# Moving two modulation pieces, one transpose block and two eviction orders in a one-core hybrid diffusion layer

## The chip, the cores and the metric

The kernel runs on one core of one Trainium2 chip. Its time is the device time of the execution in microseconds (us). Five engines work side by side: PE (TensorE, with its weight loads shown apart as PEld), DVE (VectorE), ACT (ScalarE), POOL (GpSimd) and SP (SyncE, which here only starts DMA transfers). Each engine runs its own instructions in its own order, and waits where an operand of another engine or a buffer is not ready.

Before the change three runs took 1248.82, 1251.52 and 1250.69 us, with a median of 1250.69 us.

## The reference

One layer of a diffusion backbone in float32: 512 latent tokens, 256 context tokens, width 1024. Cut to what the change touches:

```python
mod = silu(c) @ w_mod + b_mod                       # 6 x 1024: shifts, scales, gates
sh1, sc1, gt1, sh2, sc2, gt2 = split(mod, 6)
h_lat, h_ctx = modulate(x, norm1_g, sh1, sc1), modulate(ctx, norm1_g, csh1, csc1)
p_lat, p_ctx = h_lat @ w_in, h_ctx @ w_in
y_ssd = rmsnorm((ssd(conv_silu(xBC), dt) + d * xs) * silu(z), ssd_norm_g)     # 4 groups, 4 chunks of 128 tokens
y_att = window_ctx_attention(rope(q), rope(k), v, k_ctx, v_ctx, sink)
o = (sigmoid(g1) * (y_ssd @ w_o_ssd) + sigmoid(g2) * (y_att @ w_o_att)) @ w_out
x = x + gt1 * o
x = x + gt2 * (conv_ffn(modulate(x, norm2_g, sh2, sc2)))
return rmsnorm(x, final_g)
```

## The kernel before, in words

**Matrix products.** Every weight arrives as float32 in tiles of 128 x 1024 (512 KB). ACT casts such a tile to a high part (line 148, `whi<-wraw`), DVE subtracts it from the tile to get the low part (line 149, `wlo<-wraw,whi`), and activations are split in the same way. A product is then three matmuls for each of eight k blocks: lines 192 and 193 use the high weight, line 195 the low one. `gemm` walks k from 0 to 7; after k = 1, 4 and 7 it takes one function off the front of the list `BETWEEN` and runs it, which is how small work of another stage is put between the matmuls of a projection.

**Weight queue.** All weights go through one ring of three raw buffers (tag `raw`, tile `wraw`, line 144), in the order of the program. `run` asks for each weight one ahead of its use. SP issues the transfers in that order, and an issue waits until the buffer that it overwrites has been read: for a projection's weight by the subtraction of line 149, for a modulation piece by the second of its two accumulations of line 724. What follows on SP waits behind it.

**Modulation pieces.** `m_step(i)` reads a 512 KB piece of `w_mod` with two DVE operations (lines 722 or 724) that scale it by silu(c) and add it to `tm`. Every fourth piece adds four transposes on PE (line 728) and a sum on DVE (lines 730 and 731). Pieces 0 to 7 are placed in the four state-space groups (two each), 8 to 15 beside the branch projections `os_step(3)` to `os_step(7)`, 16 to 23 beside the five output projections `out_step(0)` to `out_step(4)`, and the other eight beside the feed-forward steps. `weave` spreads them evenly.

**Values.** `v_step` (line 825) forms the values and the time steps of six blocks of 128 tokens (four latent, two context) in six accumulators. For each k it runs all six blocks, so the six end together. Then ACT casts each accumulator (line 839) and copies its last 64 columns (line 841), and DVE subtracts (line 840), in the order of the blocks. The first score matmul of the attention (line 885) comes next on PE.

**State-space groups.** `ssd_steps(g)` works chunk by chunk. `chunk_out` ends with `late` (line 1541): four transposes add `dx` to the accumulator `yd` (line 1546), and DVE multiplies by the gate (line 1548, `zs`). `late` is not run at once. It is the last entry of `BETWEEN`, and `x_fn`, the projection of the next group that stands between the chunks, runs it inside its matmuls. `x_fn` itself appends two entries which transpose the convolved tile of the previous projection (`turn`, line 1346, taken out by the ACT copies of line 1389). With three empty entries ahead of it, `late` runs after k = 1 of the context half (256 tokens) of the projection, since the latent half takes the first three. The convolution of a projection is an ACT scale (1318), two DVE taps (1319, 1320), a tanh on ACT (1326) and a product on DVE (1327).

**Output projection.** `out_step(o)` needs the weight `wout` of its column block, all eight blocks of the merged branches (`mh` and `ml`, made by lines 1621 to 1624), and x. Column blocks 5 to 7 are formed last, in `out_last`, by halves of 256 tokens (lines 1691 to 1693, weights in `wlast`).

**The end.** `down_last` forms the last column block of the result by two halves. For half `u` `add` evicts it (line 1897), squares it on ACT (line 1705), sums squares by matmul (line 235), takes the root (DVE 245, POOL 246), spreads it by transposes (line 252), and `finish(u)` scales eight blocks of the result (DVE line 1880, for two of them POOL line 1878) and stores them by pairs (line 1882). The pairs alternate between SP and ACT as the engine that issues.

## Time and profile before

| view | what | value |
|---|---|---|
| run | profiled execution, its span | 1249.82 us, 1248.0 us |
| run | granted TensorE clock | 0.998 |
| page, 1 | PE busy, matmuls | 1233.6 us (99%), 6466 |
| page, 1 | DVE, ACT, POOL busy | 860.0, 655.8, 145.8 us |
| page, 4 | chain that ended last | PE 91%, DVE 4%, DMA 2% |
| stretches | 544 to 662 us (groups 1 and 2): PE busy | 116.54 of 118.00 us |
| stretches | 662 to 728 us (last group): PE busy | 66.00 of 66.00 us |
| stretches | 800 to 827 us (branch projections' end): PE busy | 27.00 of 27.00 us |
| stretches | 827 to 856 us (output projection): PE busy | 26.80 of 29.00 us |
| stretches | 827 to 856 us: DMA share, rate | 0.76, 240 GB/s |

In the view of the stretches a stage is read by itself: busy time of each engine, and how far the DMA engines were loaded. The view of waits names, for each line that stood idle, what ended the idleness. The timeline gives start, length, engine and line of each instruction; a bracket at the end of a row tells how long the engine was idle before it and what ended that.

### The profile page before, as it was taken

To read this page: it belongs to the slowest core of one execution; us is meant where nothing else is said; L and a number is where in the kernel's file an instruction comes from. 1 tells how busy PE (TensorE), PEld (TensorE's weight loads), DVE (VectorE), ACT (ScalarE), POOL (GpSimd) and SP (SyncE) were. 2 spreads that over 40 slices of the span, in tenths; PEclk is the share of its full clock that TensorE was granted. 3 is DMA by queue.
4 is the path that set the end of the run, shared out by engine and by line. 5 is a ranking of instruction groups with operands and counts; after the bars stand their busy time and mean duration, and the time that the engine had idled before them with its cause. 6 is when DMAs were issued, how large, how long until landed. Compare 5 with 4: busy or idle time off the path is not lost.

```text
span 1248.0 us, 17379 instructions
## 1 busy us (share of the span) xinstructions
PE 1233.6 (99%) x6466; PEld 1013.4 (81%) x6466; DVE 860.0 (69%) x1385; ACT 655.8 (53%) x1223; POOL 145.8 (12%) x145
## 2 busy tenths in 40 slices
PE   9999999999999999999999999999999999999997
PEld 6798888888888878777777788888888888888886
DVE  4857788888645697886977667676777767772333
ACT  4657788787445476575674752224544444442221
POOL 0000000000000152351552630000100000000000
PEclk9999999999999999999999999999999999999999
DMA  9643242222356336344365477775233333333331
GB/s 379 235 134 87 64 136 80 83 79 77 119 174 192 95 105 165 96 155 156 102 186 169 143 257 256 233 234 168 85 118 109 111 118 118 105 111 95 104 93 68
DMA packets 90997, 174.57 MB, mean 140 GB/s; under 512 B 7712, under 2 KB 43360, under 8 KB 90912
## 3 DMA queue, kind: packets, MB, share of 16 engines
q1 hardware_dynamic: 89680, 172.40, 44.1%
q8 instruction: 51, 0.84, 0.3%
q10 hardware_dynamic: 1232, 1.06, 0.2%
q14 instruction: 34, 0.28, 0.1%
HBM read 150.82 MB, written 17.11 MB: 135 GB/s over the span
## 4 chain that ended last, share of the span: by engine, by line
PE 91%; DVE 4%; DMA 2%; ACT 1%; POOL 1%; issue 1%; DVEq 0%; ACTq 0%; POOLq 0%
PE acc L192 21%; PE acc L193 21%; PE acc L195 21%; PE score L885 3%; PE po L934 3%; PE mis L524 2%; PE pt L921 2%; PE mis L1525 2%; PE mis L1430 1%; DMA wraw<-wout 1%; PE acc L1004 1%; PE acc L1005 1%; PE acc L1006 1%; PE mis L1447 1%; PE mis L1533 1%; PE acc L1821 1%
## 5 line engine op out<-in xcount | busy, mean ns | idle before, releaser
L149 DVE TENSOR_TENSOR wlo<-wraw,whi 128x1024 fp32r<-128x1024 f32 (+2 forms) x127 | 157.8, 1242 | 128.1 <-ACT whi L148 124.9
L148 ACT CAST whi<-wraw 128x1024 fp32r<-128x1024 f32 (+2 forms) x127 | 131.1, 1033 | 190.9 <-PE acc L193 147.6
L192 PE MATMUL acc<-hlh,whi 128*128 128x512 f32 x472 | 193.8, 411 | 0.0
L195 PE MATMUL acc<-hlh,wlo 128*128 128x512 f32 x472 | 185.0, 392 | 0.0
L193 PE MATMUL acc<-hll,whi 128*128 128x512 f32 x472 | 184.9, 392 | 0.0
L195 PE MATMUL acc<-mh,wlo 128*128 128x512 f32 x368 | 143.4, 390 | 0.5 <-DVE wlo L149 0.5
L192 PE MATMUL acc<-mh,whi 128*128 128x512 f32 x368 | 143.6, 390 | 0.0
L193 PE MATMUL acc<-ml,whi 128*128 128x512 f32 x368 | 143.2, 389 | 0.0
L195 PEld LDWEIGHTS acc<-hlh,wlo 128*128 128x128 f32 x472 | 88.6, 188 | 19.4
L192 PEld LDWEIGHTS acc<-hlh,whi 128*128 128x128 f32 x472 | 88.8, 188 | 17.9 <-issue 3.1
L193 PEld LDWEIGHTS acc<-hll,whi 128*128 128x128 f32 x472 | 88.9, 188 | 17.4 <-issue 2.4
L195 PEld LDWEIGHTS acc<-mh,wlo 128*128 128x128 f32 x368 | 69.1, 188 | 15.6 <-DVE wlo L149 1.2
L192 PEld LDWEIGHTS acc<-mh,whi 128*128 128x128 f32 x368 | 69.1, 188 | 14.7 <-ACT whi L148 0.4
L193 PEld LDWEIGHTS acc<-ml,whi 128*128 128x128 f32 x368 | 69.1, 188 | 14.1
L1432 POOL TENSOR_TENSOR st<-st,eT 128x512 f32<-128x512 f32 x24 | 28.9, 1203 | 440.7 <-ACT st L1449 426.4
L894 DVE CUSTOM_DVE_ANT_0 p<-score,winm,nsink 128x512 f32<-128x512 f32 (+1 forms) x64 | 51.8, 810 | 16.3 <-PE score L885 14.8
L1319 DVE SCALAR_TENSOR_TENSOR ta<-acc,half,ta 128x511 f32<-128x511 f32 (+1 forms) x66 | 43.8, 664 | 24.5 <-ACT ta L1318 24.4
L246 POOL TENSOR_TENSOR rs<-ms,phalf 128x2 f32<-128x2 f32 (+1 forms) x5 | 4.8, 956 | 478.5 <-DVE ms L245 478.5
L192 PE MATMUL acc<-fh,whi 128*128 128x512 f32 x154 | 60.0, 390 | 0.0
L193 PE MATMUL acc<-fl,whi 128*128 128x512 f32 x154 | 59.9, 389 | 0.0
L195 PE MATMUL acc<-fh,wlo 128*128 128x512 f32 x154 | 59.9, 389 | 0.0
L901 ACT ACTIVATE p<-p,mneg 128x512 f32<-128x512 f32 (+1 forms) x64 | 49.7, 777 | 16.1 <-DVE mneg L894 15.5
(377 smaller groups left out, 2888.8 us busy)
## 6 DMA issues: line engine op xcount, KB each, us to landing
wraw<-wup SPq DMA_DIRECT2D x44, 512.0 KB, 3.5
fb<-cs_d SPq DMA_DIRECT2D x32, 512.0 KB, 6.4
wraw<-wm SPq DMA_DIRECT2D x32, 512.0 KB, 3.8
wraw<-wx SPq DMA_DIRECT2D x24, 512.0 KB, 3.4
wm<-wm SPq DMA_DIRECT2D x16, 512.0 KB, 8.1
wraw<-wz SPq DMA_DIRECT2D x16, 512.0 KB, 3.5
wraw<-wos SPq DMA_DIRECT2D x16, 512.0 KB, 4.5
wraw<-wdn SPq DMA_DIRECT2D x16, 512.0 KB, 3.5
```

The source lines that it names most:

```text
L148: S.copy(hi[:, :n], r[:, :n])
L149: V.tensor_tensor(lo[:, :n], r[:, :n], raw(hi[:, :n]), ALU.subtract)
L192: T.matmul(ps, wh, xh[:, k0 + k, :], start=a, stop=False)
L193: T.matmul(ps, wh, xl[:, k0 + k, :], start=False, stop=False)
L195: T.matmul(ps, wl, xh[:, k0 + k, :], start=False, stop=b)
L524: T.matmul(ps, w[a], h[b], start=c == 1, stop=c % n == 0, skip_group_check=True)
L885: T.matmul(ps[:, o : o + len(z) * P], Q[h][:, b * P : (b + 1) * P], k[:, j, z[0] * P : (z[-1] + 1) * P], start=v == 0 and o % 512 in (0, P ...
L894: V.tensor_tensor_reduce(p[:, :w], d["ps"][i][:, o0 : o0 + w], m, op0=ALU.add, op1=ALU.min, scale=1.0, scalar=nsink[:, h : h + 1], accum_o ...
L901: S.activation(p, p, AF.Exp, bias=d["mneg"][:, i : i + 1], scale=-1.0, accum_out=d["den"][:, i : i + 1])
L934: T.matmul(d["po"], vst[:, cols[x], j, :], d[y][x], start=x == 0 and y == "pth", stop=x == c - 1 and y == "ptl")
L1319: V.scalar_tensor_tensor(o[:, 1:n], ps[:, 0 : n - 1], hcol(base_w, i), o[:, 1:n], ALU.mult, ALU.add)
L1432: G.tensor_tensor(h8(n), h8(s), bc64(eT[:, z0 : z0 + 8, c]), ALU.mult)
```

## The change

Four edits are made together. Code that comes later in the file moves down by up to 14 lines, so a line number of the kernel before answers to a slightly higher one after (1548 to 1550, 1880 to 1885).

1. `v_step` runs k = 0 to 5 over all six blocks as before, then finishes k = 6 and 7 block by block in the order 4, 5, 0, 1, 2, 3, and evicts in that order.
2. In groups 0 to 2 `late` has four empty entries ahead of it in place of three, and is one entry with `turn(1)`, followed by `turn`. So it runs after k = 4 of the context half in place of k = 1. `x_fn` adds its own entries only where the list is empty (group 0's projections), and then leaves the first place empty.
3. Group 3 takes four modulation pieces (6 to 9) in place of two. The branch projections take 10 to 17, the output projection 18 to 23: six in place of eight.
4. In `down_last` the second half's last block is evicted and squared in two pieces of 128 tokens; the first half's four stores are spread (two before the last eviction, one after it, one after the root); the second half is stored by seven transfers, all but one of a single block of 128 x 256, in the order 0, 1, 4, (2, 3), 5, 6, 7.

**PE and DVE in a chunk of a group.** The first rows are PE's before, in the context half of a projection: `late`'s transposes (1546) come after six of its 24 matmuls.

```order
L192 MATMUL acc<-hch,whi 128x256
L193 MATMUL acc<-hcl,whi 128x256
L195 MATMUL acc<-hch,wlo 128x256
L1546 MATMUL mis<-ident,dx 128x128 x4
L192 MATMUL acc<-hch,whi 128x256
L193 MATMUL acc<-hcl,whi 128x256
```

After the change they come behind nine more, directly ahead of the first `turn` (1347, formerly 1346).

```order
L192 MATMUL acc<-hch,whi 128x256
L193 MATMUL acc<-hcl,whi 128x256
L195 MATMUL acc<-hch,wlo 128x256
L1548 MATMUL mis<-ident,dx 128x128 x4
L1347 MATMUL mis<-ident,tc 128x128 x4
L192 MATMUL acc<-hch,whi 128x256
```

On DVE the gate's product `zs` stood between the two taps of the latent convolution (1319 and 1320) before:

```order
L1517 TENSOR_TENSOR E<-E,mis 128x512 x2
L1319 SCALAR_TENSOR_TENSOR ta<-acc,half,ta 128x511
L1548 TENSOR_TENSOR zs<-mis,zs 128x4x128
L1320 SCALAR_TENSOR_TENSOR ta<-acc,half,ta 128x511
L1327 SCALAR_TENSOR_TENSOR tc<-tb,ta 128x512
```

and stands behind both now:

```order
L1519 TENSOR_TENSOR E<-E,mis 128x512 x2
L1320 SCALAR_TENSOR_TENSOR ta<-acc,half,ta 128x511
L1321 SCALAR_TENSOR_TENSOR ta<-acc,half,ta 128x511
L1550 TENSOR_TENSOR zs<-mis,zs 128x4x128
L1328 SCALAR_TENSOR_TENSOR tc<-tb,ta 128x512
```

So the second tap moves ahead of the gate's product, in each of these chunks.

**SP in the output projection.** Before, from the weight of output step 2 on (`te<-xT` is the x of an output step; `wm` a modulation piece):

```order
L144 DMA wraw<-wout 128x1024
L144 DMA wraw<-wm 128x1024
L1727 DMA te<-xT 128x512
L144 DMA wraw<-wout 128x1024
L144 DMA wraw<-wm 128x1024 x2
L1727 DMA te<-xT 128x512
L144 DMA wraw<-wout 128x1024
L1727 DMA te<-xT 128x512
L144 DMA wraw<-wm 128x1024 x2
L144 DMA wraw<-wout 128x1024 x3
```

After:

```order
L144 DMA wraw<-wout 128x1024
L144 DMA wraw<-wm 128x1024
L144 DMA wraw<-wout 128x1024
L1732 DMA te<-xT 128x512
L144 DMA wraw<-wm 128x1024
L1732 DMA te<-xT 128x512
L144 DMA wraw<-wout 128x1024
L144 DMA wraw<-wm 128x1024 x2
L1732 DMA te<-xT 128x512
L144 DMA wraw<-wout 128x1024 x3
```

Between the weights of steps 2 and 4 stood three pieces, and stand two; between the weight of step 4 and the last three stand two as before.

**DVE at the end.** Before, `ms` (line 245) of the second half stands behind four scalings of the first half's blocks:

```order
L1897 SCALAR_TENSOR_TENSOR x_7544<-acc,mod_90,x_7544 128x256
L1880 SCALAR_TENSOR_TENSOR x_7544<-x_7544,vec,mis 128x256 x4
L245 TENSOR_SCALAR ms<-mis 128x2
L1880 SCALAR_TENSOR_TENSOR x_7543<-x_7543,vec,mis 128x256 x4
L1880 SCALAR_TENSOR_TENSOR x_7544<-x_7544,vec,mis 128x256 x2
```

After:

```order
L1910 SCALAR_TENSOR_TENSOR x_7553<-acc,mod_90,x_7553 128x128 x2
L1885 SCALAR_TENSOR_TENSOR x_7553<-x_7553,vec,mis 128x256 x2
L245 TENSOR_SCALAR ms<-mis 128x2
L1885 SCALAR_TENSOR_TENSOR x_7553<-x_7553,vec,mis 128x256 x2
L1885 SCALAR_TENSOR_TENSOR x_7552<-x_7552,vec,mis 128x256 x4
L1885 SCALAR_TENSOR_TENSOR x_7553<-x_7553,vec,mis 128x256 x2
```

Two of the four scalings move behind `ms`, and the eviction ahead of them is in two pieces.

```diff
@@ -825,16 +825,17 @@
     def v_step(*w):
 
         pos = [misb() for _ in range(5)] + [accb()]
-        for k in range(KT):
+
+        for k, t in [(k, t) for k in range(6) for t in range(6)] + [(k, t) for t in (4, 5, 0, 1, 2, 3) for k in (6, 7)]:
             wh, wl = (z[:, (k % 3) * 320 : (k % 3 + 1) * 320] for z in w[k // 3])
-            for t, po in enumerate(pos):
-                hh, hl, c0 = (hlh, hll, t) if t < 4 else (hch, hcl, t - 4)
-                c, o = slice(c0 * P, (c0 + 1) * P), po[:, 0:320]
-                T.matmul(o, hh[:, k, c], wh, start=k == 0, stop=False)
-                T.matmul(o, hh[:, k, c], wl, start=False, stop=False)
-                T.matmul(o, hl[:, k, c], wh, start=False, stop=k == KT - 1)
+            hh, hl, c0 = (hlh, hll, t) if t < 4 else (hch, hcl, t - 4)
+            c, o = slice(c0 * P, (c0 + 1) * P), pos[t][:, 0:320]
+            T.matmul(o, hh[:, k, c], wh, start=k == 0, stop=False)
+            T.matmul(o, hh[:, k, c], wl, start=False, stop=False)
+            T.matmul(o, hl[:, k, c], wh, start=False, stop=k == KT - 1)
         steps = tmp("te")
-        for t, po in enumerate(pos):
+        for t in (4, 5, 0, 1, 2, 3):
+            po = pos[t]
             o = po[:, 0:256].rearrange("p (h d) -> p h d", h=4)
             S.copy(vst[:, t, :, 0:64], o)
             V.tensor_tensor(vst[:, t, :, 64:128], o, raw(vst[:, t, :, 0:64]), ALU.subtract)
@@ -1377,7 +1378,8 @@
             i = 4 * g + ct
             pl, pc = accb(), accb()
             gemm([LAT(pl)], w)
-            BETWEEN.extend([lambda: turn(1), turn])
+            if not BETWEEN:
+                BETWEEN.extend([lambda: None, lambda: turn(1), turn])
             gemm([CTX(pc)], w)
             for pp, n, dst in ((pl, L, d["xs"]), (pc, LC, d["xsc"])):
                 xl = tmp("tc")
@@ -1548,7 +1550,10 @@
                 V.tensor_tensor(z, yd.rearrange("p (a t) -> p a t", a=4), z, ALU.mult)
 
             assert not BETWEEN
-            BETWEEN.extend([lambda: None] * (3 if g < 3 else 2) + [late])
+            if g < 3:
+                BETWEEN.extend([lambda: None] * 4 + [lambda: (late(), turn(1)), turn])
+            else:
+                BETWEEN.extend([lambda: None] * 2 + [late])
 
         def gate():
             for ct in range(4):
@@ -1567,7 +1572,7 @@
         s = ssd_steps(g)
         f = fill[n2 + g : n2 + 1 + g]
         b = proj_steps(g + 1) if g < 3 else fill[n2 + 4 : n3]
-        m = msteps[2 * g : 2 * g + 2]
+        m = msteps[2 * g : 2 * g + (4 if g == 3 else 2)]
 
         prog += s[0:1] + f + b[0:1] + s[1:2] + m[0:1] + b[1:2]
         for c in range(4):
@@ -1575,8 +1580,8 @@
             prog += b[2 + c : 3 + c]
             if c == 1:
                 prog += b[6:]
-            if c == 1:
-                prog += m[1:2]
+            if c == 1 or g == 3:
+                prog += m[1 + c : 2 + c] if g == 3 else m[1:2]
         prog += s[9:10]
     run(prog)
     bpool.close()
@@ -1871,7 +1876,7 @@
             if u:
                 r3s = tmp("tc")[:, :HL]
                 S.copy(r3s, rms_spread(r["s"], 2)[:, :HL])
-            for i, cs in enumerate(((0, 1), (2, 3), (4, 5), (6, 7))):
+            for i, cs in enumerate(((0,), (1,), (4,), (2, 3), (5,), (6,), (7,)) if u else ((0, 1), (2, 3), (4, 5), (6, 7))):
                 for c in cs:
                     x = x1[c // 4][:, c % 4, z]
                     if u and c in scaled:
@@ -1879,11 +1884,10 @@
                     else:
                         V.scalar_tensor_tensor(x, x, col(V_FG, c), r3[:, :HL], ALU.mult, ALU.mult)
                 n, c = len(cs), cs[0]
-                (S if i % 2 else nc.sync).dma_start(
+                tc.keep_in_program_order((S if c in ((1, 2, 6) if u else (2,)) else nc.sync).dma_start(
                     out[c * P : (c + n) * P, z].rearrange("(a p) t -> p a t", a=n), x1[c // 4][:, c % 4 : c % 4 + n, z]
-                )
-                if c == 0:
-                    yield
+                ))
+                yield
 
         def root():
             r["s"] = half_root(pf, r["sq"], 0)
@@ -1891,11 +1895,21 @@
         def spread():
             r["f"] = finish(0)
             next(r["f"])
+            next(r["f"])
 
         def add(u):
             xo = x1[1][:, 3, HALF[u]]
-            V.scalar_tensor_tensor(xo, ps[u][:, :HL], mod2[:, 31:32], xo, ALU.mult, ALU.add)
-            r["sq"] = half_squares([xo])
+            if u == 0:
+                V.scalar_tensor_tensor(xo, ps[u][:, :HL], mod2[:, 31:32], xo, ALU.mult, ALU.add)
+                r["sq"] = half_squares([xo])
+            else:
+
+                sq = tmp("tc")[:, :HL]
+                for b in range(2):
+                    z = slice(b * P, (b + 1) * P)
+                    V.scalar_tensor_tensor(xo[:, z], ps[u][:, z], mod2[:, 31:32], xo[:, z], ALU.mult, ALU.add)
+                    S.activation(sq[:, z], xo[:, z], AF.Square)
+                r["sq"] = [sq]
 
         for i, c in enumerate((4, 5)):
             scaled[c] = tmp("te")[:, :HL]
@@ -1906,19 +1920,19 @@
                 half_gemm(ps[u], F["h"], F["l"], HALF[u], w[i], (8, 8, 6)[i], 8 * i, NFF, {11: root, 17: spread} if u else {})
                 if i == 2:
                     add(u)
-            for _ in r["f"]:
-                pass
+            next(r["f"])
             r["s"] = half_root(pf, r["sq"], 1)
-            for _ in finish(1):
-                pass
+            for f in (r["f"], finish(1)):
+                for _ in f:
+                    pass
 
     run(
         [([], lambda: (y_split(range(8)), [square(True) for _ in range(4)], y_split(range(8, 12))))]
         + fill[n3:]
         + [([], zpool.close), os_first(0), ([], lambda: y_split(range(12, 16))), os_first(1)]
         + [os_step(2)]
-        + weave([os_step(o) for o in range(3, 8)], msteps[8:16])
-        + weave([out_step(o) for o in range(5)], msteps[16:24])
+        + weave([os_step(o) for o in range(3, 8)], msteps[10:18])
+        + weave([out_step(o) for o in range(5)], msteps[18:24])
         + [([], vectors)]
         + [([("out", o) for o in (5, 6, 7)], out_last), ([], close_c1)]
         + weave([up_step(t) for t in range(NFF)], msteps[24:])
```

## The prediction

> **What bounds the kernel now.** I read the page first: busy times, and the chain that ended last.
>
> ```profile
> PE 1233.6 (99%) x6466; PEld 1013.4 (81%) x6466; DVE 860.0 (69%) x1385; ACT 655.8 (53%) x1223; POOL 145.8 (12%) x145
> PE 91%; DVE 4%; DMA 2%; ACT 1%; POOL 1%; issue 1%; DVEq 0%; ACTq 0%; POOLq 0%
> ```
>
> PE is busy for 1233.6 of 1248.0 us. No edit takes a matmul away, so all that can be won lies in 14.4 us of idle PE, the end included, and a little behind it, because a matmul that follows a stall also starts slowly. The view of waits for PE names where that idle time lies:
>
> ```profile
> PE mis L252 <- POOL rs L246: 1.3, 1, 1.3
> PE mis L235 <- ACT tc L1705: 1.3, 1, 1.3
> PE acc L1693 <- DVE wlast L149: 0.8, 1, 0.8
> PE score L885 <- ACT te L841: 0.7, 1, 0.7
> PE mis L728 <- DVE tm L724: 0.6, 1, 0.6
> PE acc L195 <- DVE wlo L149: 0.5, 1, 0.5
> PE mis L1546 <- POOL dx L1538: 0.5, 1, 0.5
> PE mis L1430 <- ACT xsc L1389: 0.4, 1, 0.4
> PE acc L1691 <- ACT wlast L148: 0.3, 1, 0.3
> PE mis L1493 <- ACT xsc L1389: 0.3, 1, 0.3
> PE mis L1525 <- DVE zs L1548: 0.2, 1, 0.2
> ```
>
> Each row is one wait. Four of them (1693, 728, 195, 1691) are the output projection's: 0.8 + 0.6 + 0.5 + 0.3 = 2.2 us, the largest sum. The first two belong to the end, 885 to the values, the others to the state-space groups. The edits touch just these four places. The profiled execution took 1249.82 us, 1.82 us more than its span; it lies 0.87 us below the median of the three runs, 1250.69.
>
> **Values.** The timeline before the first score:
>
> ```profile
> 95.55 0.31 PE L834 MATMUL acc<-wlo,hch 128*128 128x320 f32 x1
> 95.70 0.31 PE L835 MATMUL acc<-whi,hcl 128*128 128x320 f32 x1
> 96.04 0.37 ACT L839 CAST vst<-acc 128x256 fp32r<-128x256 f32 x1
> 96.73 0.38 PE L885 MATMUL score<-khi,q 128*128 128x256 f32 x1 [0.72 <-ACT te L841]
> ```
>
> The score waits 0.72 us for the copy out of a `mis` buffer, the fifth block's, behind ACT's queue of six casts and copies. After the change that block is finished first, with 5 blocks x 6 matmuls behind it. A matmul of 320 columns starts 0.15 us after the one ahead (95.55 to 95.70), so 4.4 us lie between the block's last matmul and the first score; its cast needs 0.37 us and the copy of 64 columns less. The wait goes. From 95.70 to 96.73 are 1.03 us, 0.88 more than 0.15: beside the wait of 0.72 a stall costs 0.16 us of slow start, which I add to other waits below. The next eviction that PE can meet, the last block's, is used no earlier than the values' products behind the softmax. I take 0.8 us; lower end 0.5 (a score waits for another buffer), upper end 0.9.
>
> **Groups 0 to 2.** In the timeline, the last chunk of group 2, where `late` waits:
>
> ```profile
> 653.86 0.28 PE L193 MATMUL acc<-hcl,whi 128*128 128x256 f32 x1
> 653.98 0.28 PE L195 MATMUL acc<-hch,wlo 128*128 128x256 f32 x1
> 654.77 0.66 PE L1546 MATMUL mis<-ident,dx 128*128 128x128 f32 x4 [0.51 <-POOL dx L1538]
> ```
>
> and two chunks in which `zs` is what PE needs next, the second of group 1 and the second of group 2:
>
> ```profile
> 551.21 0.68 DVE L1548 TENSOR_TENSOR zs<-mis,zs 128x512 f32<-128x512 f32 x1
> 551.81 0.74 DVE L1320 SCALAR_TENSOR_TENSOR ta<-acc,half,ta 128x511 f32<-128x511 f32 x1
> 551.95 1.13 PE L1525 MATMUL mis<-st,CT 128*128 128x512 f32 x2 [0.20 <-DVE zs L1548]
> 554.53 1.13 PE L1430 MATMUL mis<-xw,Bk 128*128 128x512 f32 x2 [0.43 <-ACT xsc L1389]
> ```
>
> and
>
> ```profile
> 631.88 0.68 DVE L1548 TENSOR_TENSOR zs<-mis,zs 128x512 f32<-128x512 f32 x1
> 632.74 1.09 PE L1533 MATMUL mis<-E,xs 128*64 128x128 f32 x16
> ```
>
> `late` moves behind nine matmuls of 256 columns. They start 0.12 us apart (653.86 to 653.98), so it comes 1.08 us later, more than the 0.51 us by which `dx` was late: 0.51 + 0.16 = 0.67 us gained. The price is on DVE: `zs` now stands behind the second tap, 0.6 us later (551.81 less 551.21, one place in the queue). Where PE already waited for it (551.95, the buffer that `zs` frees), the stall grows from 0.20 to about 0.9 us: minus 0.7. In the other chunk `zs` ends at 632.56 and PE uses the buffer at 632.74, 0.2 us to spare: minus 0.4. In return the tap, and with it the tanh and the copies of line 1389, come 0.6 us earlier, so the waits for `xsc` (0.43 and 0.31) go: with slow starts 0.59 + 0.47 = 1.06. Sum: 0.67 + 1.06 - 1.1 = 0.6. Ends: 1.5 (`zs` costs next to nothing) and minus 0.5 (the waits for `xsc` stay, 0.67 - 1.1).
>
> **Output projection.** The chain of waits runs through the weight ring:
>
> ```profile
> 829.47 4.71 DMA wraw<-wout
> 834.27 1.06 ACT whi L148
> 835.36 1.24 DVE wlo L149
> 836.61 5.90 DMA wraw<-wout
> 846.39 4.30 DMA wraw<-wout
> 800.00:827.00 27.00, 27.00 (x122) 22.32 (x121) 20.30 (x30) 6.07 (x7) 0.00 (x0) 1.00 0.70 221
> 827.00:856.00 29.00, 26.80 (x129) 21.30 (x129) 21.37 (x30) 9.08 (x11) 0.00 (x0) 1.00 0.76 240
> ```
>
> The last two rows, of the stretches, have PE, PEld, DVE, ACT and POOL busy, then clock, DMA share and rate: no PE idle before 827, 2.2 us of it behind, and the DMA not full. What limits is the ring of three. A buffer is taken for load, cast and subtraction: 4.3 to 5.9 + 1.06 + 1.24, so 6.6 to 8.2 us. Three buffers pass one load in 2.2 to 2.7 us. A step is 24 matmuls of about 0.22 us (27.00 by 122), 5.3 us. Before, five steps ask for 5 weights and 8 pieces: 2.6 loads a step, one in 2.0 us, more than the ring passes. After, 11 loads: 2.2 a step, one in 2.4 us, inside the band. Step 4's weight, issued at 836.61 when step 3's subtraction had freed its buffer, should go out some 2 us earlier, since only one piece stands between the weights of steps 2 and 3, and of 3 and 4. Its low part came at 842.6 + 1.06 + 1.24 = 844.9, 0.5 us too late for PE; 2 us earlier it is not. The first of the last three weights now takes over the buffer of step 4's (three places back in the queue), free at about 842.9: + 4.3 + 1.06 + 1.24 = 849.5. PE wants it one step behind 844.4, at 849.7 or a little earlier. So the four waits go but for a rest. They cost 2.2 + 4 x 0.16 = 2.8 us; I take 2.3; ends 0.3 and 2.8.
>
> Two pieces move into group 3, where PE has no idle time:
>
> ```profile
> 662.00:728.00 66.00, 66.00 (x316) 47.54 (x315) 43.87 (x66) 37.22 (x86) 29.96 (x30) 1.00 0.48 150
> L724 DVE SCALAR_TENSOR_TENSOR tm<-wraw,csil,tm x14: 731/749/1580, 406.9 to 686.6; 128x512 f32<-128x512 f32 x14
> ```
>
> Four DVE operations of 0.75 us, two transfers and one set of transposes that is only placed earlier. DVE is idle for 22 of the 66 us and the DMA half of the time, so they hide: cost nothing, and at worst, each at the maximum of the second row, 4 x 1.58 = 6.3 us of DVE time, still inside the 22 idle.
>
> The maximum stands where POOL works beside DVE. [...] What that could cost is a rival below.
>
> **The end.** From the timeline:
>
> ```profile
> 1238.44 0.40 ACTq L1882 DMA_DIRECT2D out<-x  x1
> 1238.72 1.65 DVE L1880 SCALAR_TENSOR_TENSOR x<-x,vec,mis 128x256 f32<-128x256 f32 x4
> 1238.94 0.42 ACT L1705 ACTIVATE tc<-x 128x256 f32<-128x256 f32 x1 [5.51 <-DVE x L1897]
> 1239.41 0.60 PE L235 MATMUL mis<-rmsc,tc 128*128 128x1 f32 x4 [1.26 <-ACT tc L1705]
> 1240.28 0.15 DVE L245 TENSOR_SCALAR ms<-mis 128x2 f32<-128x2 f32 x1
> ```
>
> The split square wins nothing: ACT is held by its issue until 1238.84 anyway. But `ms` stood behind four scalings, which end at 1240.37, while its sums were ready at 1239.41 + 0.60 = 1240.01; with two ahead it is free: 0.25 us. Scalings leave 0.40 us apart (1.65 for four), so the first store can start 0.40 us earlier as a single block. The last store carries 128 KB in place of 256 KB. Against that stand three more issues of 0.40 us each, spread over two queues, of which the last on SP (block 7 behind 5) may be late by one. I take 0.5; ends minus 0.4 (one issue more on the path) and 0.9 (0.25 + 0.40 and a shorter last transfer).
>
> **Sum.** 0.8 + 0.6 + 2.3 + 0.5 = 4.2 us. Against its own execution: 1249.82 - 4.2 = 1245.6; against the median: 1246.5. I take the middle, 1246.0.
>
> **Rivals.**
>
> *The ring stays short.* The two pieces removed only bring the demand to the upper part of the band; if loads take 5.9 us, the ring passes one in 2.7 us, and a stall remains at step 4 and at `wlast`. For it: the three transfers in the chain are already far apart in length, 4.30 to 5.90. Against: the DMA share falls as two of 13 loads go. The gain there is then 0.3: 0.8 + 0.6 + 0.3 + 0.5 = 2.2, 1248.5 against the median.
>
> *The gate's product pays for `late`.* The delay of `zs` hits twelve chunks, and I priced only two. For it: the row at 551.95 shows PE waiting on just this product. Against: it is a single wait of 0.2 us in the view. With minus 0.5 in place of 0.6 the sum is 3.1: 1247.6.
>
> *The moved pieces disturb group 3.* If each of the four operations holds POOL for 0.75 us or is held for 0.83 (1.58 - 0.75), and POOL's products for `dx` reach PE late, 4 x 0.8 = 3.2 us of the gain is lost: sum 1.0, 1249.7, no measurable change. Against: PE waits there for nothing, and DVE has 22 us free. [...]
>
> *A lost turn of the ring, slower.* In the new order the last piece of the branch projections stands on DVE ahead of the eviction of their last step (line 1621), from which the merged branches are made that every output step needs. If its load lands more than about 1.5 us behind that step's last matmul, the whole output projection starts late. At one full turn, 8.2 us less 1.5, that costs 6.7 us; with the gains of the other three edits, 1.9, it gives 1250.69 + 6.7 - 1.9 = 1255.5. For it: the stretch before has the same DMA load. Against: PE was not idle between 800 and 827 us, where as many pieces run.
>
> **How the numbers follow.** Forecast 0.58; ring stays short 0.19; gate's product 0.12; group 3 0.06; lost turn 0.05. The forecast's own range is 1244.0 to 1247.6, from the terms' ends and the spread of the runs. For 8 in 10 it reaches to the ring's case: 1243.0 to 1249.4. A change under 0.2% (2.5 us) can't be told from none in these runs: faster means below 1248.2. Faster: 0.58 + 0.12 + somewhat under half of 0.19, 0.78; same: the rest of that and group 3, 0.17; slower 0.05.
>
> **What would show it.** In the profile after: no wait of 885 for ACT; no wait of 1548 (`late`) for `dx`, but a longer one of 1527 for `zs`, and none for `xsc`; in the output projection PE idle under 1 us in place of 2.2, the transfer of step 4's weight issued about 2 us earlier against PE's matmuls; group 3 still without idle PE; `ms` directly behind its sums, and a last store of a single block. Wrong would make it: a wait for `wlo` or `wlast` of the old size, a first output step that waits for `mh` or `ml`, or PE idle between 662 and 728 us.

## The result and the profile after

The changed kernel takes 1244.45 us (median of 6 runs, 1242.91 to 1246.14), against 1250.65 us (6 runs, 1248.82 to 1252.39) for the kernel before in the same comparison: a ratio of 0.9949, with a 95% interval of 0.9937 to 0.9962. That is 6.2 us or 0.5% faster. The forecast was 1246.0. The profiled execution took 1244.75 us with a span of 1243.0, 5.0 us less than before.

The page of the changed kernel, busy times and the chain that ended last:

```profile
PE 1232.2 (99%) x6466; PEld 1014.6 (82%) x6466; DVE 863.8 (69%) x1386; ACT 655.3 (53%) x1224; POOL 145.5 (12%) x145
PE 94%; DVE 2%; ACT 1%; DMA 1%; POOL 1%; issue 0%; DVEq 0%; ACTq 0%; POOLq 0%
```

PE does the same 6466 matmuls, and less of the chain runs through DVE and DMA (DVE 4% to 2%, DMA 2% to 1%). The view of waits for PE, changed kernel, all rows:

```profile
PE mis L235 <- ACT tc L1911: 1.1, 1, 1.1
PE mis L252 <- POOL rs L246: 1.1, 1, 1.1
PE mis L410 <- DVE ones L393: 1.0, 1, 1.0
PE mis L1535 <- ACT tb L1327: 1.0, 1, 1.0
PE acc L480 <- DVE csil L398: 0.7, 1, 0.7
```

Gone are the values' wait (885 before), the four of the output projection, and the groups' waits for `dx`, `xsc` and `zs`. One wait of 1.0 us is new (1535). The stretches, changed kernel (PE, PEld, DVE, ACT, POOL busy, then clock, DMA share, GB/s):

```profile
662.00:728.00 66.00, 66.00 (x316) 47.72 (x315) 47.36 (x71) 38.05 (x87) 29.44 (x30) 1.00 0.56 172
827.00:856.00 29.00, 29.00 (x164) 25.30 (x163) 22.24 (x31) 10.29 (x13) 0.00 (x0) 1.00 0.73 234
```

The last group carries two more pieces (DVE 43.87 to 47.36 us, DMA share 0.48 to 0.56), and PE is still busy in all of it. In the output projection PE has no idle time left (26.80 of 29.00 us before), at the same rate of the DMA engines: 234 GB/s, 240 before.

Where the time went is seen best by laying the two traces side by side, the nth matmul of one against the nth of the other. How much PE won (minus) or lost in a stage, in us, in one profiled execution each:

| kernel (edits) | before 30 us | values, 30 to 110 | groups, 110 to 660 | 740 to 870 |
|---|---|---|---|---|
| changed | +1.55 | -0.97 | -1.34 | -3.63 |
| changed, run again | -0.06 | -0.97 | -1.35 | -3.63 |
| 1 and 4 alone | -0.21 | -0.97 | +0.24 | -1.25 |
| 3 alone | +0.38 | +0.01 | +0.20 | -3.63 |
| 2 alone | -0.42 | 0.00 | -1.07 | +1.25 |
| 1, 3, 4 | -0.44 | -0.98 | +1.28 | -3.63 |
| changed, stores by pairs | +0.04 | -0.97 | -1.95 | -3.63 |
| changed, `late` at its old place in every third chunk | -0.37 | -0.98 | -1.49 | -3.63 |

The last column is the output projection. The first two rows agree in every stage but the first, whose 1.55 us belongs to the execution. Rows for code that an edit did not touch show the scatter of a stage: up to 1.3 us in the groups and in the output projection. All rows are set against one execution of the kernel before, so its own scatter is in every row. In the output projection two other executions of the old code took 1.25 us less and 1.25 us more than it; against these, edit 3 is worth 2.4 and 4.9 us.

### The profile page after: what moved, and what is told of

Read it like the earlier page. It is cut to its first block, busy times and chain, and to the rows that moved or that the text cites. A ratio compares the mean times of both kernels' runs of the same rounds, so it can differ in the third digit from the quotient of the medians.

```text
span 1243.0 us, 17390 instructions
## 1 busy us (share of the span) xinstructions
PE 1232.2 (99%) x6466; PEld 1014.6 (82%) x6466; DVE 863.8 (69%) x1386; ACT 655.3 (53%) x1224; POOL 145.5 (12%) x145
## 4 chain that ended last, share of the span: by engine, by line
PE 94%; DVE 2%; ACT 1%; DMA 1%; POOL 1%; issue 0%; DVEq 0%; ACTq 0%; POOLq 0%
PE acc L192 22%; PE acc L195 22%; PE acc L193 22%; PE score L886 3%; PE po L935 3%; PE mis L524 2%; PE pt L922 2%; PE mis L1527 2%; PE mis L1432 1%; PE acc L1005 1%; PE acc L1006 1%; PE acc L1007 1%; PE mis L1449 1%; PE mis L1535 1%; PE acc L1826 1%; PE mis L1347 1%
## 5 line engine op out<-in xcount | busy, mean ns | idle before, releaser
L1319 ACT ACTIVATE ta<-acc,half 128x512 f32<-128x512 f32 (+1 forms) x66 | 46.9, 710 | 21.9 <-PE acc L195 20.5
```

The costliest lines, as they stand in the source:

```text
L1319: S.activation(o[:, :n], ps[:, :n], AF.Identity, scale=hcol(base_w, stride + i), bias=hcol(base_b, i))
```

## Experiments

### Each edit by itself

The first four kernels take the change apart. Values and end alone (edits 1 and 4):

```diff
-        for k in range(KT):
+        for k, t in [(k, t) for k in range(6) for t in range(6)] + [(k, t) for t in (4, 5, 0, 1, 2, 3) for k in (6, 7)]:
...
+            for i, cs in enumerate(((0,), (1,), (4,), (2, 3), (5,), (6,), (7,)) if u else ((0, 1), (2, 3), (4, 5), (6, 7))):
```

> Edits 1 and 4 alone (values block by block, the end by blocks). Theory: the terms stand alone; values 0.8 us and end 0.5 us, so 1250.65 - 1.3 = 1249.35; in the trace no wait of the score matmul for ACT, while the waits of the state-space groups and of the output projection are all there as before (2.2 us of PE idle in the output projection). Rival: the end's 0.5 us needs nothing but its own stores, but the score's wait only moves, to the values' products: then 1250.1.

Measured: 1248.35 us against 1250.31, ratio 0.9986 (0.9977 to 0.9996). The score's wait is gone. Of the four waits of the output projection, whose code is that of before, the 0.5 us at 195 was missing in this execution.

The pieces alone (edit 3):

```diff
-        m = msteps[2 * g : 2 * g + 2]
+        m = msteps[2 * g : 2 * g + (4 if g == 3 else 2)]
...
-        + weave([os_step(o) for o in range(3, 8)], msteps[8:16])
-        + weave([out_step(o) for o in range(5)], msteps[16:24])
+        + weave([os_step(o) for o in range(3, 8)], msteps[10:18])
+        + weave([out_step(o) for o in range(5)], msteps[18:24])
```

> Edit 3 alone (two modulation pieces moved into the last group). Theory of the weight ring: the four waits of the output projection go, and about 3.6 us with them (that is what the offset of PE against the kernel before grows by in this stage in the changed kernel): 1247.05, with no PE idle in the last group. Rival: part of the 3.6 us came from the other edits (the stage started 0.8 us earlier against its transfers): then 2.3 us, 1248.3, and waits of 1 us remain. Second rival: the last group pays, PE idle between 662 and 728 us.

Measured: 1246.19 us, 0.9969 (0.9959 to 0.9979). All four waits of the output projection are gone, and PE has no idle time in the last group.

`late` alone (edit 2):

```diff
-            BETWEEN.extend([lambda: turn(1), turn])
+            if not BETWEEN:
+                BETWEEN.extend([lambda: None, lambda: turn(1), turn])
...
-            BETWEEN.extend([lambda: None] * (3 if g < 3 else 2) + [late])
+            if g < 3:
+                BETWEEN.extend([lambda: None] * 4 + [lambda: (late(), turn(1)), turn])
```

> Edit 2 alone (late by three k blocks, with the first turn). Theory: the groups give 1.5 us (the growth of the offset there in the changed kernel): 1249.15; no wait of late for dx, none for xsc, and one new wait of about 1 us in the third chunk of group 2, ahead of the products of E and xs. Rival: that new wait is chance of one execution and is absent here; then 2.5 us, 1248.15. The output projection keeps its 2.2 us of idle PE.

Measured: 1248.52 us, 0.9992 (0.9983 to 1.0000): not told from no change by time, though the trace shows 1.07 us won in the groups. In this execution the output projection, whose code is that of before, lost them again; the section on the hardware comes back to it.

All but `late` (the lines above taken back from the changed kernel, so that edits 1, 3 and 4 are left):

```diff
-            if not BETWEEN:
-                BETWEEN.extend([lambda: None, lambda: turn(1), turn])
+            BETWEEN.extend([lambda: turn(1), turn])
```

> All edits but the second. Theory: the terms add, 0.8 + 3.6 + 0.5 = 4.9 us, 1245.75, which is 1.3 us above the changed kernel; waits for dx, xsc and zs in the groups as in the kernel before. Rival: the groups' gain was chance; then as fast as the changed kernel, 1244.45.

Measured: 1245.86 us, 0.9965 (0.9951 to 0.9978). The three parts (1 and 4, 3, 2) are worth 2.0, 4.1 and 1.8 us by their medians, 7.9 in all, and 1.75, 3.9 and 1.0 by their ratios, 6.6 in all, against 6.2 for the whole. They add up within their intervals; the output projection is the largest part, as forecast, and larger than forecast (edit 3 alone: 2.6 to 5.1 us by its interval).

### Why the output projection gained: the number of loads?

The prediction explained the waits by a rate: 13 loads in five steps (five weights, eight pieces) are more than three buffers pass, 11 are just few enough. Three kernels change the number. With eight pieces in a buffer of their own:

```diff
-        r = wpool.tile([P, 1024], F32, tag="raw", name="wraw", bufs=3)
+        if key[0] == "m" and 16 <= key[1] < 24:
+            r = OWN[0].tile([P, 1024], F32, tag="rawm", name="wrawm", bufs=1)
+        else:
+            r = wpool.tile([P, 1024], F32, tag="raw", name="wraw", bufs=3)
```

> The kernel before, all eight pieces left beside the output projection, but these eight loaded into a buffer of their own (512 KB more), so that the weights have the ring of three for themselves. Same transfers, same bytes, same DVE work. Theory of the ring: the four waits go without moving a piece, about 3.5 us: 1246.8. Rival, the DMA rate (0.76 of its engines busy): the transfers are no fewer, so most of the 2.2 us of idle PE stays: 1250.

Measured: 1263.16 us against 1252.14, 1.0095 (1.0073 to 1.0116), slower. One of the rows of PE's waits is far longer here than all others:

```profile
PE mis L732 <- DVE tm L728: 11.7, 2, 10.4
```

PE waits here for no weight, but for the pieces themselves: the transposes of a set (732, formerly 728) stand in PE's order, and the pieces, one after the other through a single buffer, are read too late for them. So the time of this kernel says nothing of the ring, but its trace does. With the ring for themselves the weights of steps 2 and 4 go out at 818.56 and 826.18, against 825.79 and 836.61 before, and up to PE's first wait in this stage (844.1) the weights of steps 0 to 3 are ready 3.0 to 3.6 us ahead of their use. It is the pieces in the ring that make the weights late. Whether by their number or by the time for which they hold a buffer, this kernel can't tell: only three pieces go out between 816 and 845 us, where seven did before.

With seven pieces in the output projection (12 loads), three in the last group:

```diff
-        + weave([os_step(o) for o in range(3, 8)], msteps[8:16])
-        + weave([out_step(o) for o in range(5)], msteps[16:24])
+        + weave([os_step(o) for o in range(3, 8)], msteps[9:17])
+        + weave([out_step(o) for o in range(5)], msteps[17:24])
```

> The kernel before with one piece moved into the last group in place of two: 12 loads in the output projection, 2.4 a step, one in 2.2 us, the lower edge of what the ring passes (2.2 to 2.7). Theory of the ring: about half of the gain, 1.8 us, 1248.5; waits remain at the last weights. Rival: a single wait is the seed of the others, and goes with one piece: all 3.5 us, 1246.8.

Measured: 1251.43 us, 1.0004 (0.9993 to 1.0015), no gain. The stretch of its output projection, before with 13 loads stood at 26.80:

```profile
827.00:856.00 29.00, 26.49 (x126) 20.96 (x125) 21.21 (x30) 8.54 (x11) 0.00 (x0) 1.00 0.75 247
```

With ten pieces (15 loads), six beside the branch projections:

```diff
+        + weave([os_step(o) for o in range(3, 8)], msteps[8:14])
+        + weave([out_step(o) for o in range(5)], msteps[14:24])
```

> The kernel before with ten pieces beside the output projection and six beside the branch projections: 15 loads in five steps, 3.0 a step. Theory of the ring: each of the two further loads costs a pass of 2.2 to 2.7 us, 4.4 to 5.4 us, 1255; with so much idle PE the granted clock falls to 0.50 for some microseconds in this stage, 1 to 2 us more. Rival: the lighter stage before it gives the ring a lead that absorbs them: 1250.3.

Measured: 1251.47 us, 0.9997 (0.9988 to 1.0007). Its stretch:

```profile
827.00:856.00 29.00, 26.27 (x112) 20.35 (x112) 22.24 (x32) 7.22 (x9) 0.00 (x0) 0.94 0.74 233
```

The stretch is followed by the longest of PE's waits for a weight in this kernel:

```profile
PE acc L192 <- ACT whi L148: 2.1, 1, 2.1
```

and one of 0.5 us for `wlo`. 12, 13 and 15 loads give the same time; at 11 the waits are gone. A rate alone would have shown as a slope: half the gain at 12, several us lost at 15. So the number of loads alone does not set the time. It is not out of the picture either. With 15 loads two pieces stand ahead of each weight, and the weights of steps 2 to 5 go out 7.3, 7.1 and 8.7 us apart, 2.4 to 2.9 us per load, while PE needs some 5.5 us for a step: here the waits fit the rate. In the profiled execution, the second slowest of ten, PE lost 2.6 us more than before between 740 and 870 us. That the median shows no loss may come from the stage ahead, which has two loads fewer; that was the rival on record, and no run excludes it. And the kernel with 12 loads changed more than the number, as the next section shows.

### What held the ring

The timeline of the kernel before, around the place where the branch projections end, PE, DVE and SP:

```profile
813.80 0.33 SPq L144 DMA_DIRECT2D wraw<-wm  x1
...
820.68 0.60 PE L728 MATMUL mis<-ident,tm 128*128 128x128 f32 x4
820.88 0.69 DVE L1621 TENSOR_TENSOR tb<-acc,ld 128x512 f32<-128x512 f32 x1 [1.67 <-PE acc L195]
...
823.89 0.68 DVE L1624 TENSOR_TENSOR ml<-tb,mh 128x512 fp32r<-128x512 f32 x1
824.50 0.48 DVE L722 TENSOR_SCALAR tm<-wraw,csil 128x512 f32<-128x512 f32 x1
825.01 2.33 DVE L724 SCALAR_TENSOR_TENSOR tm<-wraw,csil,tm 128x512 f32<-128x512 f32 x3
825.79 0.33 SPq L144 DMA_DIRECT2D wraw<-wout  x1
...
831.23 1.23 DVE L149 TENSOR_TENSOR wlo<-wraw,whi 128x1024 fp32r<-128x1024 f32 x1 [1.79 <-ACT whi L148]
832.51 0.50 PE L195 MATMUL acc<-mh,wlo 128*128 128x512 f32 x1
```

Read it from the load at 813.80. This is piece 16, the first of a set of four. Its first operation (722) starts a new sum in `tm`, and there is a single `tm`: it has to wait until the transposes of the set before (728, 820.68) have read it. By then DVE has the merge of the last branch step ahead of it (1621 to 1624), so 722 runs at 824.50. Until piece 16 has been read, at 825.01 + 0.75 = 825.76, its buffer is held, for 12 us, though a transfer of a piece takes some 4 (4.1 us, the median of the four issued around here). Step 2's weight goes out at 825.79, just when this buffer is free. Its low part is ready at 832.46, and PE uses it at 832.51: no lead is left. Step 3's weight has 2.0 us again, step 4's, with two pieces ahead of it, is 0.5 us late, and that is PE's first wait. The same places of the changed kernel:

```profile
808.95 0.60 PE L728 MATMUL mis<-ident,tm 128*128 128x128 f32 x4
812.77 0.48 DVE L722 TENSOR_SCALAR tm<-wraw,csil 128x512 f32<-128x512 f32 x1
...
820.36 0.33 SPq L144 DMA_DIRECT2D wraw<-wout  x1
...
826.86 1.22 DVE L149 TENSOR_TENSOR wlo<-wraw,whi 128x1024 fp32r<-128x1024 f32 x1 [0.15 <-ACT whi L148]
832.11 0.39 PE L195 MATMUL acc<-mh,wlo 128*128 128x512 f32 x1
```

With two pieces more placed ahead of it, the set that ends with piece 15 is complete two steps earlier. Its transposes stand at 808.95, piece 16 is read at 812.77, step 2's weight goes out at 820.36 and is ready 4.0 us ahead of its use (828.08 to 832.11). The others have 3.7 and 3.4 us.

In the kernel with 12 loads the transposes of that set come at 820.85, as late as before. Piece 16 goes out earlier there and is held for 19.1 us (807.29 to 826.35), and step 2's weight follows at 826.37, again without a lead. So this kernel took one load away and held a buffer longer. In that with 15 the same set ends inside the output projection, at 827.30; piece 16 is held for 8.9 us, step 2's weight has a lead of 1.7 us, and the waits come at steps 3 to 5. A long hold costs nothing by itself: the changed kernel holds piece 20, the first of the next set, for 12.6 us (823.10 to 835.75), and with leads of 3.4 us and more no wait follows. The late end of the set thus takes away the lead at step 2, and what the loads behind it need decides whether PE waits. Two more kernels ask for the part of the single `tm`. Before, with eight pieces kept where they were, and a sum tile of its own for pieces 16 to 19:

```diff
-                macc[0] = tmp("tm")
+                macc[0] = OWN[0].tile([P, 512], F32, tag="tm2", name="tm2", bufs=1) if cg == 4 else tmp("tm")
```

> The kernel before with all eight pieces where they were, but the sum of pieces 16 to 19 in a tile of its own (2 KB a partition), so that piece 16, the first of its four, need not wait until PE has transposed the sum of the four before it. Its two DVE operations then stand ahead of the last branch step's eviction in place of behind its merge. Theory of the single sum (new, after the one-piece and ten-piece runs): piece 16 sat in the ring for that wait and took its place from the weights; without it the lead stays and the waits of the output projection shrink, by 2 to 3.5 us, 1247 to 1248.3. Theory of the ring's rate (13 loads are too many): all four waits stay, 1250.5.

Measured: 1249.01 us against 1251.04, 0.9987 (0.9978 to 0.9995). No wait for an output weight is left, with 13 loads, but PE's waits have two new rows:

```profile
PE acc L194 <- DVE ml L1626: 0.7, 1, 0.7
PE acc L193 <- ACT mh L1625: 0.5, 1, 0.5
```

and the timeline of this kernel, DVE and SP, shows where they come from:

```profile
819.38 0.48 DVE L723 TENSOR_SCALAR tm<-wraw,csil 128x512 f32<-128x512 f32 x1
...
823.68 0.75 DVE L725 SCALAR_TENSOR_TENSOR tm<-wraw,csil,tm 128x512 f32<-128x512 f32 x1 [3.03 <-DMA wraw<-wm]
824.35 0.68 DVE L1623 TENSOR_TENSOR tb<-acc,ld 128x512 f32<-128x512 f32 x1
...
827.47 0.33 SPq L144 DMA_DIRECT2D wraw<-wout  x1
```

Piece 16 is now read at 819.38, 5 us earlier. But piece 17 stands on DVE ahead of the last branch step's merge and waits for its load, 3.03 us, and the merge behind it comes late. This is the rival of a lost turn of the ring in small: 1.2 us of PE's waits in place of 2.2. The trace wins 1.60 us here, not 3.63. The run shows that the single `tm` held piece 16: with a sum of its own its buffer is taken for 6.2 us in place of 12.0 (814.45 to 820.65). It doesn't show that this hold caused the waits. Step 2's weight goes out at 827.47, later than before, since the weight whose buffer it takes is now split behind that wait of DVE. Its lead is 1.2 us, and PE is itself 1.7 us later there than in the kernel before.

The other kernel has the change's order in the branch and output projections, and leaves the last group as it was:

```diff
-        + weave([os_step(o) for o in range(3, 8)], msteps[8:16])
-        + weave([out_step(o) for o in range(5)], msteps[16:24])
+        + weave([os_step(o) for o in range(3, 8)], msteps[8:18])
+        + weave([out_step(o) for o in range(5)], msteps[18:24])
```

> The kernel before with the two pieces moved beside the branch projections (ten there, six beside the output projection) in place of into the last group, which keeps two. Piece 16 then comes two places earlier, as in the changed kernel. Theory of the single sum: the output projection has no waits, 3.5 us, 1247, if the branch projections carry ten pieces without a wait of their own. Rival: the load has to go somewhere with free transfers, and waits of 1 us or more appear in the branch projections.

Measured: 1248.76 us, 0.9979 (0.9971 to 0.9988). The transposes come at 810.21, no wait for a weight is left, and PE wins 3.37 us between 740 and 870 us. By its ratio the kernel wins 2.6 us (1.5 to 3.6). So the place in the last group is not needed for this gain: ten pieces also fit beside the branch projections, with as many loads in the two stages together as before.

What stays open: in each kernel that won the 3.6 us (3.37 in the last one) the set ended early and the output projection had 11 loads. No run had 11 loads with the set ending late, or 13 at their usual pace with the set ending early. That the pieces in the ring make the weights late is shown; how much of it comes from the late end and how much from the two loads more isn't separated.

### The end's stores, and `late` in one chunk

The changed kernel with the second half stored by pairs:

```diff
-            for i, cs in enumerate(((0,), (1,), (4,), (2, 3), (5,), (6,), (7,)) if u else ((0, 1), (2, 3), (4, 5), (6, 7))):
+            for i, cs in enumerate(((0, 1), (2, 3), (4, 5), (6, 7))):
...
-                tc.keep_in_program_order((S if c in ((1, 2, 6) if u else (2,)) else nc.sync).dma_start(
+                tc.keep_in_program_order((S if c in ((2, 6) if u else (2,)) else nc.sync).dma_start(
```

> The changed kernel with the second half's stores by pairs again (four transfers), the rest of edit 4 kept. From the start of the last matmul of the down projection to the end of the span it is 10.13 us in the kernel before, 9.59 in the changed one. Theory: the order of ms gives half, the single stores half, so 9.85 and a time 0.25 us above the changed kernel. Rivals: all by ms (9.6), all by the stores (10.1).

Measured: 1243.70 us against 1252.14, 0.9941 (0.9926 to 0.9955), not worse than the changed kernel by time. From the last matmul of the down projection to the end of the span are 10.04 us, against 9.97 in the second execution of the changed kernel (below), whose last four transposes (252) took nearly as long (1.12 and 1.11 us): by the trace the single stores are worth 0.1 us there.

The changed kernel with `late` at its old place in every third chunk:

```diff
-            if g < 3:
+            if g < 3 and c == 2:
+                BETWEEN.extend([lambda: None] * 3 + [late, lambda: turn(1), turn])
+            elif g < 3:
```

> The changed kernel, with late at its old place in the third chunk of groups 0 to 2. Theory: the wait of 1.03 us ahead of the products of E and xs in group 2 comes from the gate's product standing behind both taps; it goes, 1.0 us, 1243.4. Rival: the wait is for E itself (the masks on DVE and ACT come late): then it stays, 1244.45, or dx waits come back.

Measured: 1243.08 us against 1249.68, 0.9949 (0.9937 to 0.9962). Beside it the changed kernel was run again, without an edit:

> The changed kernel once more, beside the one above. Its first profile was 1.45 us behind the kernel before at 9 us, ahead of any edit. Theory: that is the spread of the first transfers and not part of the change: here within 0.4 us; the wait of 1 us in the third chunk of group 2 is there again. Rival: the lag belongs to the program: 1.4 us again.

Measured: 1243.71 us, 0.9953 (0.9939 to 0.9967). The timeline of PE, DVE and ACT in the kernel with the old place in the third chunk, and then PE's of the changed kernel in this run:

```profile
643.19 1.12 PE L1527 MATMUL mis<-st,CT 128*128 128x512 f32 x2 [0.18 <-DVE E L1519]
643.78 0.68 DVE L1550 TENSOR_TENSOR zs<-mis,zs 128x512 f32<-128x512 f32 x1
644.61 1.09 PE L1535 MATMUL mis<-E,xs 128*64 128x128 f32 x16 [0.29 <-DVE zs L1550]
645.21 0.63 ACT L1327 ACTIVATE tb<-ta 128x512 f32<-128x512 f32 x1 [1.66 <-DVE ta L1321]
```

```profile
645.10 1.09 PE L1535 MATMUL mis<-E,xs 128*64 128x128 f32 x16 [0.91 <-ACT tb L1327]
```

The new wait of the changed kernel, 0.91 us, becomes 0.18 + 0.29. That fits a price of the later `late`, but its size varies with the execution: the kernel with stores by pairs, whose code is the changed kernel's in this chunk, waited 0.38 us only, and the kernel with edits 1, 3 and 4, with `late` at its old place throughout, waited 0.29 for `zs` there too. The 0.6 us between the medians lie inside the intervals, and in the groups as a whole the kernel with the old place won 1.49 us, between 1.35 and 1.95 for executions of the changed code: no gain is shown.

## Why the prediction was right, and where not

**Values: right.** The forecast was 0.8 us, between 0.5 and 0.9; every execution with edit 1 won 0.97 or 0.98, a little above the upper end. The timeline of the changed kernel:

```profile
97.25 0.31 PE L835 MATMUL mis<-whi,hll 128*128 128x320 f32 x1
97.40 0.28 PE L886 MATMUL score<-khi,q 128*128 128x256 f32 x1
```

The score now starts 0.15 us behind the last matmul, the distance of two neighbours. The remaining 0.1 us is the slow start, priced too low: before, the second score came 0.22 us behind the first (96.73 to 96.95), where 0.12 is the distance undisturbed.

**Groups: right in sign, the step on `zs` wrong.** The sum was 0.6, its upper end 1.5; measured were 1.07, 1.34, 1.35 and 1.95 us in four executions with edit 2, against a loss of 0.1 to 0.2 in most executions without the edit (1.28 in one). The waits for `dx` and `xsc` went as forecast. But `zs` was to cost 0.7 us more at 551.95 and 0.4 at 632.74, and neither came. At the first place, ACT before, and ACT and DVE after:

```profile
549.21 0.63 ACT L1410 ACTIVATE sq<-zs 128x512 f32<-128x512 f32 x1 [1.79 <-POOL ssq L1411]
549.75 0.76 ACT L1318 ACTIVATE ta<-acc,half 128x512 f32<-128x512 f32 x1
```

```profile
548.29 0.76 ACT L1319 ACTIVATE ta<-acc,half 128x512 f32<-128x512 f32 x1
549.26 0.63 ACT L1412 ACTIVATE sq<-zs 128x512 f32<-128x512 f32 x1 [0.21 <-POOL ssq L1413]
550.54 0.68 DVE L1550 TENSOR_TENSOR zs<-mis,zs 128x512 f32<-128x512 f32 x1
```

Before, the scaling that feeds both taps stood on ACT behind a square that waited 1.79 us for POOL. After, it stands ahead of that square. The scaling comes 1.5 us earlier, and `zs`, though behind both taps, ends at 551.22 in place of 551.89. I had moved `zs` one place back in DVE's queue and left ACT's order as it was. Where ACT's order gave no such help, in the third chunk of group 2, which I hadn't priced, the cost did come (changed kernel):

```profile
645.20 0.75 DVE L1321 SCALAR_TENSOR_TENSOR ta<-acc,half,ta 128x511 f32<-128x511 f32 x1
645.87 0.68 DVE L1550 TENSOR_TENSOR zs<-mis,zs 128x512 f32<-128x512 f32 x1
646.70 1.09 PE L1535 MATMUL mis<-E,xs 128*64 128x128 f32 x16 [1.03 <-ACT tb L1327]
```

PE starts 0.15 us after `zs` has ended (646.55). The row names ACT's `tb`, which ends later, at 646.67. The wait is that for the buffer which `zs` frees: `tb` is no operand of this matmul, and in the kernel with `late` at its old place there the same matmul starts at 644.61, 0.15 us after `zs` and before `tb` has even begun (645.21). In all six executions in which it waits at this place it starts 0.14 or 0.15 us after `zs`. The wait was 1.03, 0.91 and 1.08 us in three executions with the later `late` and 0.38 in a fourth; in the two of the six with `late` at its old place it was 0.29. That the costs came to about the 1.1 us forecast in the first three is luck, since neither place that was priced had any. The gain was larger than the sum: the `zs` wait of 0.20 went as well, and the four waits that went, 1.45 us, less the new one of 1.03, are only 0.42 of the 1.34 us. The rest would be slow starts; no run here separates them from the scatter of the stage.

**Output projection: the waits right, the cause half seen, the size too small.** That the four waits go, and that step 4's weight goes out some 2 us earlier, came true (833.91 against 836.61, of which 0.8 us is PE's own shift). The step that failed is the time for which a buffer is taken: "load, cast and subtraction", 6.6 to 8.2 us, holds for weights, and a piece has neither cast nor subtraction. It is held until DVE can add it to the sum, 12.0 us for piece 16. So the rate, 2.2 to 2.7 us per load, does not explain by itself why 12 loads gain nothing, though at 15 loads the weights do follow each other at 2.4 to 2.9 us per load. How much of the waits is the hold and how much the number of loads stays open. The sum was mis-sized too: 2.3 us with an upper end of 2.8, measured 3.63 in each of the six executions with edit 3, against the one execution before. In that execution the four waits are 2.2 us, so 1.4 us are the slow starts: 0.36 per stall, where I had taken 0.16 from a single place. PE's timeline before, at step 4's weight:

```profile
843.34 0.39 PE L195 MATMUL acc<-mh,wlo 128*128 128x512 f32 x1
843.71 0.50 PE L192 MATMUL acc<-mh,whi 128*128 128x512 f32 x1
844.05 0.40 PE L193 MATMUL acc<-ml,whi 128*128 128x512 f32 x1
844.97 0.50 PE L195 MATMUL acc<-mh,wlo 128*128 128x512 f32 x1 [0.52 <-DVE wlo L149]
845.31 0.39 PE L192 MATMUL acc<-mh,whi 128*128 128x512 f32 x1
```

Undisturbed, matmuls start 0.23 us apart. From 843.34 to 845.31 are 1.97 us for four steps, 1.05 more than 0.92, while the only bracket says 0.52. A short delay at 843.71 has no bracket of its own, and behind each of the two delayed matmuls the next one starts 0.34 us later.

**The moved pieces: right.** They cost nothing in the last group: PE is busy for 66.00 of 66.00 us. The rival that they disturb this group has no support here. It counted a loss at each meeting of a piece's operation with POOL. In the profile before, seven operations of line 724 ran beside a POOL operation: two took 1.55 and 1.58 us (432.02 and 478.66), the other five at most 0.75. A POOL product for `dx` that met one of these five took 1.67 us (686.83), against 1.29 to 1.30 for those with DVE idle. In the last group one of the operations took 1.60 us beside a POOL operation in one execution, and none took more than 0.77 in the five others with four pieces there; PE was busy throughout in all six.

**The end: right for `ms`, less for the stores.** The forecast was 0.5. From the sums' matmuls (235) to the transposes (252) were 1.92 to 1.94 us in all eight executions with the old end and are 1.69 or 1.70 in all six with the new one; 0.25 was forecast for `ms`. The split square, priced at nothing, is worth 0.1 us: the last projection matmul and line 235 lie 1.52 to 1.54 us apart with it whole, 1.42 or 1.43 with it split. In the changed kernel:

```profile
1234.48 0.51 ACT L1911 ACTIVATE tc<-x 128x128 f32<-128x128 f32 x2 [5.51 <-DVE x L1910]
1234.84 0.61 PE L235 MATMUL mis<-rmsc,tc 128*128 128x1 f32 x4 [1.15 <-ACT tc L1911]
1235.49 0.16 DVE L245 TENSOR_SCALAR ms<-mis 128x2 f32<-128x2 f32 x1 [0.24 <-PE mis L235]
1236.54 0.65 PE L252 MATMUL mis<-ident,rs 128*128 128x128 f32 x4 [1.09 <-POOL rs L246]
```

`ms` now waits for its sums, no longer for scalings. How long it takes from line 252 to the end of the span goes with the time of these transposes. Where the four took 0.65 to 0.73 us (granted clock 1.00 in the changed kernel, 0.79 in the kernel before), it was 6.7 us with the old stores and 6.4 with the new. Where they took 1.1 us, it was 6.93 with pairs, the changed kernel with pairs among them, and 6.85 with single stores. One execution with the old stores, in which they took 0.99 us, lies between, at 6.80. So the new stores bring 0.1 to 0.25 us, of the 0.40 that I had for an earlier first store, and only the 0.1 is shown for the single stores alone.

**The sum.** From the last matmul of the down projection to the end of the span are 10.13 us before and 9.55 after, 0.58 less. 0.97 + 1.34 + 3.63 + 0.58 is 6.5 us, against 4.2 forecast; the difference lies in the output projection (1.3) and the groups (0.7). The profiled execution lost 1.55 us of it at its start, which leaves the 5.0 by which its span is shorter. The likeliest case was the one that came, at a time of 1244.45 in place of 1246.0, near the lower end of its range (1244.0).

## What to carry to other kernels

Where several streams share a ring of buffers, ask for each load not only how long it takes, but what its consumer waits for: a single sum tile that other work has yet to read can hold a buffer for 12 us where its transfer takes some 4. Test a rate by a dose, and see in the trace of each dose that nothing else has moved: here the kernel with one load fewer held a buffer for 19 us, so its flat time said less than it seemed to. And price a stall by the distance of the matmuls around it, not by the bracket alone; in the one execution of the kernel before that was 0.9 us on average for 0.55 in the output projection.

## What the runs showed of the hardware

**A lower clock can follow short stalls.** In the kernel with `late` alone the same four waits as before (0.5, 0.6, 0.4 and 0.8 us within 10 us) were followed by a lower granted clock. Its stretches of one us:

```profile
851.00:852.00 1.00, 0.68 (x5) 0.68 (x6) 1.00 (x3) 0.35 (x1) 0.00 (x0) 0.92 0.80 291
852.00:853.00 1.00, 1.00 (x6) 1.00 (x6) 0.79 (x2) 1.00 (x2) 0.00 (x0) 0.50 0.80 283
```

PE looks fully busy at 0.50 of its clock, with 6 matmuls in a us, for some three us, and the stage lost 1.25 us. In the stretch of the kernel with 15 loads, at 0.94, the clock fell too: it was 0.90 between 840 and 850 us, where PE was busy for 7.29 us of 10, and 0.93 between 850 and 860. The kernel before kept 1.00 over 827 to 856 us with nearly the same waits, so the fall comes in some executions only; that the waits cause it is not shown.

**The first 9 us vary.** The changed kernel's PE was 1.55 us behind before's in one execution and 0.06 us ahead in the next, with the same code there, so a difference of 1.5 us between two single profiles can lie wholly in the first 9 us. The first weight landed only 0.3 us later (4.74 against 4.45 us). The rest is matmuls that start further apart, 22 in place of 33 between 5 and 9 us at a granted clock of 1.00 in both; why, these runs do not show.
